# Layer-2 projections of a two-layer decoder computed as 30 block pairs by seven half-size products, with two spills to DRAM

## The chip, the cores and the metric

One core of a Trainium2 chip runs the whole program. The metric is the device time of one execution in microseconds; lower is better. PE is the matrix engine, PEld its weight loader, DVE, ACT and POOL are the vector, scalar and GpSimd engines, SP the engine that issues most transfers.

## The reference, cut to what matters

A decoder of two layers on 512 tokens of width 2048, all in f32. Layer 1 is a sparse attention with a token indexer; layer 2 is a stick-breaking attention against one K and V made from layer 1's output `x`. Each layer ends with an output projection, a layer norm and a gated embedding. The part that the change touches:

```
kb, vb = split(x @ w_kv_b)                 # 2048 x 4096: 16 heads of 128 columns each for K and V
q, g   = split(x @ w_q_b)                  # 2048 x 4096: Q and the gate, 16 heads each
z = q k^T * 128^-0.5                       # per head, strictly causal
a = exp(log_sigmoid(z) + reverse cumsum of log_sigmoid(-z) behind it)
y = ((a @ v) * silu(g)) @ w_out_b
x = layer_norm(4^0.25 * x + y);  x = x + (p @ w_ple) * sigmoid(x @ w_ple_gate)
```

## The kernel before, in words

Activations are held transposed: 16 tiles `xT[m]` of 128 features by 512 tokens. To keep f32 accuracy each operand is split in two fp32r parts, a high one (`h`, `wh`, a rounded copy by ACT) and a low one (`l`, `wl`, the rest, by DVE), and every product is three matmuls, high by high, high by low, low by high (`mm3`, lines 88 to 93). A matmul of the projections has a 128x128 block of weights loaded first and then 512 columns of tokens.

The projections are a list of chunks. A chunk is one weight tile `raw` of 128x1024 (512 KB), loaded by SP, split into `wh` and `wl` (`split_w`, L161 and L162), and used by 24 matmuls. There are 4 `raw` buffers and 3 pairs of `wh` and `wl`. At the start of chunk c the program issues the split of chunk c+2 and the load of chunk c+6 (`ahead`). A block (`block`) is two columns of 128 weights, that is two heads' worth or a head's K and Q: 4 chunks, 96 matmuls, two PSUM tiles of 128x512 in `g` buffers. `natural_block` makes V for four heads with tokens on the partitions: 8 chunks.

In layer 2 (lines 767 to 794) the loop over 16 heads emits for each four heads one `natural_block` for V, for each two heads a block for the gates, and for each head a block for K and Q. When the results are done, `b_done` splits them. The attention of a head is queued (`slots`) and one piece is taken out after each chunk: `stick_tile` for four tiles of 128 queries (scores on PE, two sigmoids on ACT, two triangular masks on POOL, a scan and a product on DVE), ten transposes (L441), and the product with V, whose gated result `u[h]` stays on chip until the output projection `mix_out(1)`. The 16 tiles `xT[m]` of layer 1's output stay on chip as `h` and `l` for the whole of layer 2; `out_done` adds them back from there. All order is fixed by the program text: each engine takes its instructions in that order and waits on semaphores.

Of the kernel before, what the change touches and what calls it, by code (L numbers as in the profile page):

```python
# [12 lines left out]
P = 128  # L13
# [18 lines left out]
RAW_BUFS = 4  # L32
HL_BUFS = 3
T_BUFS = 78

# [10 lines left out]
class Chunk:  # L46
    def __init__(self, loads, mms, pre=None, after=None, pops=1):
        self.pops = pops
        self.mid = None
        self.loads = loads  # L50
        self.mms = mms
        self.pre = pre
        self.after = after


class Kernel:
    def __init__(self, tc, pools):
# [23 lines left out]
    def split(self, src, w=T, lo=0):  # L81
# [4 lines left out]
        return h, l  # L86

# [60 lines left out]

    def load(self, c):
        if c < len(self.chunks):  # L150
            ch = self.chunks[c]
            ch.raw = self.raw.tile([P, 1024], F32, tag="raw", name=self.name("raw"))
            ch.loads(ch.raw)

    def split_w(self, c):
        if c < len(self.chunks):
            ch = self.chunks[c]
            nc = self.nc
            ch.h = self.hl.tile([P, 1024], F32R, tag="wh", name=self.name("wh"))
            ch.l = self.hl.tile([P, 1024], F32R, tag="wl", name=self.name("wl"))  # L160
            nc.scalar.copy(ch.h, ch.raw)  # L161
            nc.vector.tensor_tensor(ch.l, ch.raw, ch.h.bitcast(F32), op=OP.subtract)  # L162
            ch.raw = None

    def ahead(self, c):
        self.split_w(c + HL_BUFS - 1)
        self.load(c + RAW_BUFS + HL_BUFS - 1)

    def run(self):
        self.prologue()  # L170
        for c in range(len(self.chunks)):
# [4 lines left out]
            if ch.pre:  # L176
                ch.pre()
            for n, (off, out, xs) in enumerate(ch.mms):
# [25 lines left out]
def body(tc, x, p, positions, w_in_a, w_out_a, w_q_b, w_kv_b, w_out_b, ln_g, ln_b, w_ple, w_ple_gate, freq, out):  # L204
    nc = tc.nc
    with tc.tile_pool(name="const", bufs=1) as const, \
            tc.tile_pool(name="raw", bufs=RAW_BUFS) as raw, \
            tc.tile_pool(name="hl", bufs=HL_BUFS) as hl, \
            tc.tile_pool(name="t", bufs=T_BUFS) as tp, \
            tc.tile_pool(name="psum", bufs=1, space=bass.MemoryType.PSUM) as psum, \  # L210
            tc.manual_schedule():
        k = Kernel(tc, (const, raw, hl, tp, psum))
# [4 lines left out]
def _emit(k, x, p, positions, w_in, w_out_a, w_q, w_kv, w_out_b, ln_g, ln_b, w_ple, w_gate, freq, out):  # L217
# [43 lines left out]
    pos = const.tile([P, T], F32, name="pos")  # L261
# [171 lines left out]
    def tail(h, a):  # L433
# [16 lines left out]
        def stage_v():  # L450
            o = k.ps("o")
            sl = slice(a["col"] * P, (a["col"] + 1) * P)
            for j in range(NT):
                vh, vl = a["v"][j]
                k.mm3(o[:, j * P:T], (vh[:, sl], vl[:, sl]), a["pt"][j], j == 0, j == NT - 1)
# [64 lines left out]

    def q_done_a(h, i, ps):
        a = att.setdefault(h, {"p": [None] * NT})
        if i == 0:
            rope(ps, st[0], 64, lambda r: a.__setitem__("q", k.split(r)))
            a["k"], a["v"], a["col"] = kx[h // 4], va, h // 4
# [14 lines left out]
    def prologue():  # L540
        for n in range(RAW_BUFS):
            load_x(n)
            k.load(n)
            if n == 1:
                load_small()
        for n in range(RAW_BUFS, 8):
            load_x(n)
        first_x(range(2))
        k.split_w(0)
        k.load(RAW_BUFS)  # L550
        k.split_w(1)
        k.load(RAW_BUFS + 1)
# [115 lines left out]

    def ln_apply(layer, ms):
# [38 lines left out]
    def mix_out(layer):  # L708
# [4 lines left out]
        for n, (b, kc) in enumerate(order):  # L713
            if b not in outs:
                outs[b] = [Out(KT, lambda ps, m=2 * b + i: out_done(m, ps)) for i in range(2)]
            pre = None
            if n == 6:
                pre = finish
            if n == 0:
                k.chunks[-3].after = lambda: us_ahead(0)  # L720
                k.chunks[-2].after = lambda: us_ahead(1)
            k.chunks.append(k.chunk4(view, (2 * b * P, (2 * b + 1) * P), kc, outs[b], us, pre=pre, pops=1))
            if n in (1, 5):
                k.chunks[-1].after = lambda n=n: us_ahead(2 if n == 1 else 3)
# [30 lines left out]

    def x1_fin(m, v):
        xT[m] = k.split(v)
# [4 lines left out]

    mix_out(0)
    ple_chunks(0)
    gate_block(0, x1_fin)

    def b_done(h, what, ps):
        a = att.setdefault(100 + h, {"p": [None] * NT})
        if what == "g":
            sg = k.tt(s="sg")  # L770
            nc.scalar.activation(sg, ps, AF.Sigmoid)
            nc.vector.tensor_tensor(sg, sg, ps, op=OP.mult)
            a["g"] = sg
            return
        a[what] = k.split(ps)
        if what == "q":
            a["v"], a["col"] = vb[h // 4], h % 4
            slots(a, h, stick_tile)

    def b_load(h):  # L780
        def loads(raw, kc):
            r = raw.rearrange("p (k c) -> p k c", k=4)
            nc.sync.dma_start(r[:, :, 0:P], wkv_v[:, 4 * kc:4 * kc + 4, h * P:(h + 1) * P])
            nc.sync.dma_start(r[:, :, P:2 * P], wq_v[:, 4 * kc:4 * kc + 4, h * P:(h + 1) * P])

        return loads
# [11 lines left out]
    def out_fin(m, v):  # L798
        k.defer(lambda: out_store(m, v))
# [48 lines left out]
```

## Time and profile before

| | |
|---|---|
| median of 3 runs | 2180.03 us (2179.91 to 2180.98) |
| the profiled execution | 2180.3 us, its span 2178.5 us |
| PE busy, share of the span | 99%, 10081 matmuls |
| weight loads busy | 83% |
| DVE, ACT, POOL busy | 52%, 38%, 8% |
| DMA, mean | 92 GB/s |
| granted PE clock | 9 tenths or more in all 40 slices |

A matmul's row lasts longer than the distance to the next row's start, since matmuls overlap in the engine: what a matmul costs a stream is the distance of starts, not its length. In the projections of layer 2, from 1064 to 1815 us of the span, PE has no idle time in the windows view.

### The profile page before, as it was taken

To read this page: it belongs to the slowest core of one execution; us is meant where nothing else is said; L and a number is where in the kernel's file an instruction comes from. 1 tells how busy PE (TensorE), PEld (TensorE's weight loads), DVE (VectorE), ACT (ScalarE), POOL (GpSimd) and SP (SyncE) were. 2 spreads that over 40 slices of the span, in tenths; PEclk is the share of its full clock that TensorE was granted. 3 is DMA by queue.
4 is the path that set the end of the run, shared out by engine and by line. 5 is a ranking of instruction groups with operands and counts; after the bars stand their busy time and mean duration, and the time that the engine had idled before them with its cause. 6 is when DMAs were issued, how large, how long until landed. Compare 5 with 4: busy or idle time off the path is not lost.

```text
span 2178.5 us, 25725 instructions
## 1 busy us (share of the span) xinstructions
PE 2159.6 (99%) x10081; PEld 1803.0 (83%) x10081; DVE 1141.0 (52%) x1759; ACT 824.6 (38%) x1271; POOL 170.1 (8%) x227
## 2 busy tenths in 40 slices
PE   8999999999999999999999999999999999999999
PEld 7987888888888887888888888888888888887887
DVE  4576976555566458543344434434443456548532
ACT  3564345455553236332233323322332343226322
POOL 6101000000001010000010000100000010100000
PEclk9999999999999999999999999999999999999999
DMA  6333332223222322333323222232233222332431
GB/s 199 107 90 84 99 86 78 78 74 82 78 88 88 100 93 78 107 97 97 97 78 97 87 87 87 79 96 86 80 94 90 88 87 88 96 98 76 125 117 58
DMA packets 263946, 201.21 MB, mean 92 GB/s; under 512 B 12752, under 2 KB 251408, under 8 KB 263824
## 3 DMA queue, kind: packets, MB, share of 16 engines
q1 hardware_dynamic: 263824, 199.56, 30.4%
q8 instruction: 79, 1.29, 0.2%
q14 instruction: 43, 0.35, 0.1%
HBM read 195.33 MB, written 4.19 MB: 92 GB/s over the span
## 4 chain that ended last, share of the span: by engine, by line
PE 94%; DVE 3%; ACT 1%; issue 0%; DMA 0%; SPq 0%; ACTq 0%
PE g L91 29%; PE g L93 29%; PE g L92 29%; PE s L441 2%; PE s L91 1%; PE o L93 1%; PE o L92 1%; PE s L93 1%; PE s L92 1%; PE o L91 1%; DVE z L674 1%; PE s L375 1%; DVE z L673 1%; DVE wl L162 1%; ACT wh L161 0%
## 5 line engine op out<-in xcount | busy, mean ns | idle before, releaser
L91 PE MATMUL g<-h,wh 128*128 128x512 f32 (+1 forms) x2576 | 1003.9, 390 | 3.4 <-ACT h L84 3.4
L92 PE MATMUL g<-l,wh 128*128 128x512 f32 (+1 forms) x2576 | 997.3, 387 | 3.6 <-DVE l L85 3.6
L93 PE MATMUL g<-h,wl 128*128 128x512 f32 (+1 forms) x2576 | 997.2, 387 | 0.5 <-DVE wl L162 0.5
L162 DVE TENSOR_TENSOR wl<-raw,wh 128x1024 fp32r<-128x1024 f32 x362 | 448.6, 1242 | 503.5 <-ACT wh L161 501.1
L91 PEld LDWEIGHTS g<-h,wh 128*128 128x128 f32 x2576 | 484.2, 188 | 103.3 <-ACT h L84 5.4
L92 PEld LDWEIGHTS g<-l,wh 128*128 128x128 f32 x2576 | 484.2, 188 | 99.9 <-DVE l L85 5.9
L161 ACT CAST wh<-raw 128x1024 fp32r<-128x1024 f32 x362 | 380.1, 1054 | 492.8 <-PE g L92 384.8
L93 PEld LDWEIGHTS g<-h,wl 128*128 128x128 f32 x2576 | 483.9, 188 | 97.0 <-DVE wl L162 1.0
L91 PE MATMUL g<-wh,h 128*128 128x512 f32 x320 | 126.5, 395 | 2.1 <-ACT wh L161 2.1
L92 PE MATMUL g<-wl,h 128*128 128x512 f32 x320 | 125.2, 391 | 0.5 <-DVE wl L162 0.5
L93 PE MATMUL g<-wh,l 128*128 128x512 f32 x320 | 125.3, 392 | 0.0
L513 POOL TENSOR_SCALAR_AFFINE_SELECT keep<-keep 128x128 f32<-128x128 f32 x64 | 20.1, 314 | 931.3 <-ACT keep L509 772.1
L85 DVE TENSOR_TENSOR l<-s,h 128x512 fp32r<-128x512 f32 (+1 forms) x116 | 64.7, 611 | 50.5 <-ACT h L84 50.5
L509 ACT ACTIVATE keep<-s 128x128 f32<-128x128 f32 (+1 forms) x64 | 28.2, 441 | 159.0 <-PE s L93 157.8
L516 DVE TENSOR_TENSOR_SCAN r<-keep,zeros 128x127 f32<-128x127 f32 (+1 forms) x64 | 54.6, 853 | 56.4 <-POOL keep L513 56.4
L501 ACT ACTIVATE pr<-pr,s 128x128 f32<-128x128 f32 (+1 forms) x64 | 36.2, 566 | 125.9 <-DVE s L500 125.6
L84 ACT CAST h<-s 128x512 fp32r<-128x512 f32 (+1 forms) x116 | 54.2, 539 | 64.6 <-PE s L278 31.7
L318 POOL TENSOR_TENSOR rb<-rb,sin 128x512 f32<-128x512 f32 (+2 forms) x29 | 36.0, 1240 | 475.4 <-ACT rb L316 320.2
L91 PEld LDWEIGHTS g<-wh,h 128*128 128x128 f32 x320 | 60.5, 189 | 14.6 <-ACT wh L161 2.5
L92 PEld LDWEIGHTS g<-wl,h 128*128 128x128 f32 x320 | 60.5, 189 | 13.2 <-DVE wl L162 1.0
L93 PEld LDWEIGHTS g<-wh,l 128*128 128x128 f32 x320 | 60.4, 189 | 12.7
L85 DVE TENSOR_TENSOR l<-g,h 128x512 fp32r<-128x512 f32 x52 | 35.9, 691 | 60.6 <-ACT h L84 60.6
(151 smaller groups left out, 1633.7 us busy)
## 6 DMA issues: line engine op xcount, KB each, us to landing
raw<-in_w_in_a_dram SPq DMA_DIRECT2D x132, 256.0 KB, 3.2
raw<-in_w_ple_gate_dram SPq DMA_DIRECT2D x64, 512.0 KB, 3.5
raw<-in_w_in_a_dram SPq DMA_DIRECT2D x32, 512.0 KB, 4.1
raw<-in_w_out_a_dram SPq DMA_DIRECT2D x32, 512.0 KB, 3.5
raw<-in_w_kv_b_dram SPq DMA_DIRECT2D x32, 512.0 KB, 3.7
raw<-in_w_q_b_dram SPq DMA_DIRECT2D x32, 512.0 KB, 3.7
raw<-in_w_kv_b_dram SPq DMA_DIRECT2D x64, 256.0 KB, 2.9
raw<-in_w_q_b_dram SPq DMA_DIRECT2D x64, 256.0 KB, 3.3
```

The source lines that it names most:

```text
L84: nc.scalar.copy(h[:, lo:w], src[:, lo:w])
L85: nc.vector.tensor_tensor(l[:, lo:w], src[:, lo:w], h.bitcast(F32)[:, lo:w], op=OP.subtract)
L91: nc.tensor.matmul(out, ah, bh, start=start, stop=False)
L92: nc.tensor.matmul(out, ah, bl, start=False, stop=False)
L93: nc.tensor.matmul(out, al, bh, start=False, stop=stop)
L161: nc.scalar.copy(ch.h, ch.raw)
L162: nc.vector.tensor_tensor(ch.l, ch.raw, ch.h.bitcast(F32), op=OP.subtract)
L318: nc.gpsimd.tensor_tensor(b[:rows, col:], b[:rows, col:], sin[:rows, col:], op=OP.mult)
L441: nc.tensor.transpose(banks[b][:, off + (i - j) * P:off + (i - j + 1) * P], a["p"][i][:, j * P:(j + 1) * P], ident)
L501: nc.scalar.activation(pr[:, :n], pr[:, :n], AF.Exp, bias=mx, scale=1.0, accum_out=sm)
L509: nc.scalar.activation(keep[:, :n], ps[:, :n], AF.Sigmoid, scale=-SCALE)
L516: nc.vector.tensor_tensor_scan(r[:, 0:n - 1][:, ::-1], keep[:, 1:n][:, ::-1], zeros.to_broadcast([P, n - 1]), 1.0, op0=OP.mult, op1=OP.add)
```

## The change

The 30 pairs of 128-column blocks (16 K with Q for heads 0 to 15, two pairs of gates for heads 0 to 3, 12 V with gate for heads 4 to 15) are each computed by a scheme of seven products instead of eight (`quads`). The contraction is cut in even and odd feature tiles, the tokens in two halves of 256. Each product is one chunk of 24 matmuls of 256 columns (8 feature tiles, three matmuls each). Its weight tile is a sum of up to four quarter blocks, built in place in a `raw` buffer: four quarters are loaded by SP, two additions per pair are made by accumulating transfers that POOL issues (`add_load`), and two by DVE (`add_plus`). The token side's sums are made once from layer 1's output by `make_forms` and kept on chip as fp32r forms `F` (seven of them, 8 tiles each); an eighth, A21, serves only the one V block for heads 0 to 3, which stays a `natural_block` of its own kind (`natural_halves`). The products are added up in three PSUM tiles A, B and E, with three additions on DVE and four copies on ACT per pair. V of heads 4 to 15 comes out transposed and is turned by four PE transposes per head (`b_values`).

To make room, layer 1's output is stored to DRAM after it is made (`x1_store`) and loaded again for the residual, two tiles per block of `mix_out(1)` (`x1_load`), and `u[h]` of heads 0 to 13 is stored (`u_store`) and loaded in the last pair (`u_load`). `raw` has 6 buffers, and `plan` sets when each split, addition and load is issued. The attention of a head is no longer queued but tied to given products of the next pairs. The output tiles are stored one chunk later (`defer_by(1, ...)`).

```diff
-RAW_BUFS = 4
+HALF = T // 2
+RAW_BUFS = 6
+KEEP_U = 14
+LOAD_LEAD = 6
+ADD_LEAD = 5
...
+    def multiply(self, ch, ps, xs, start, stop):
+        nc = self.nc
+        for j in range(KT // 2):
+            wh, wl = (z[:, j * P:(j + 1) * P] for z in (ch.h, ch.l))
+            xh, xl = xs(j)
+            for n, (a, b) in enumerate(((wh, xh), (wl, xh), (wh, xl))):
+                nc.tensor.matmul(ps[:, :HALF], a, b, start=start and j == 0 and n == 0,
+                                 stop=stop and j == KT // 2 - 1 and n == 2, skip_group_check=True)
...
+        def after7(q):
+            q.setdefault("s17", None) or q.__setitem__("s17", self.tt(s="s17"))
+            nc.scalar.copy(q["s17"][:, HALF:], q["E"][:, :HALF])
...
+        def after2(q):
+            q["o1"] = self.tt(s="o1")
+            nc.vector.tensor_tensor(q["o1"][:, :HALF], q["s17"][:, :HALF], q["B"][:, :HALF], op=OP.add)
...
+            product(q, "P7", "S3", "E", True, False, after7, fresh=(1, c2), add=(0, c2))
+            if last:
+                product(q, "P1", "A11", "A", True, False, after1, fresh=(0, c1))
+                third(last)
+            product(q, "P6", "S2", "A", False, False, after6, grown=q["P7"], plus=q["P1"])
+            product(q, "P2", "A12", "B", True, True, after2, fresh=(1, c1))
+            product(q, "P4", "A22", "E", False, True, after4, grown=q["P6"], plus=q["P2"])
+            product(q, "P5", "S1", "A", False, False, after5, add=(0, c2), grown=q["P1"])
+        third(qs[-1])
...
+    def add_load(self, c):
+        ch = self.chunks[c]
+        if ch.grown is not None:
+            ch.raw = ch.grown.raw
+        self.nc.gpsimd.dma_start(ch.raw.rearrange("p (k c) -> p k c", k=8), ch.add, accum_op=OP.add)
+
+    def add_plus(self, c):
+        ch = self.chunks[c]
+        ch.raw = ch.grown.raw
+        self.nc.vector.tensor_tensor(ch.raw, ch.raw, ch.plus.raw, op=OP.add)
...
+            ch.split_at = c - HL_BUFS + 1
...
+                ev(c - LOAD_LEAD - (2 if ch.add else 0), 3, c, self.load)
...
+                t = max(ch.grown.split_at, ch.plus.split_at)
+                assert t < ch.split_at
+                ev(t, 1, c, self.add_plus)
...
+            if ch.add and ch.grown is None:
+                ev(c - ADD_LEAD, 2, c, self.add_load)
+            elif ch.add:
+                ev(ch.grown.last[0], 2, c, self.add_load)
...
+        if m in x1:
+            nc.vector.scalar_tensor_tensor(z, x1.pop(m), ALPHA, ps, op0=OP.mult, op1=OP.add)
...
-        if what == "q":
-            a["v"], a["col"] = vb[h // 4], h % 4
-            slots(a, h, stick_tile)
...
-    for h in range(HEADS):
-        if h % 4 == 0:
-            vb[h // 4] = {}
-            k.natural_block(wkv_v, D + h * P, xs, lambda t, ps, v=vb[h // 4]: v_done(v, t, ps))
-        if h % 2 == 0:
-            k.block(wq_v, (D + h * P, D + (h + 1) * P), xs, lambda i, ps, h=h: b_done(h + i, "g", ps))
-        k.block(None, b_load(h), xs, lambda i, ps, h=h: b_done(h, "kq"[i], ps))
...
+        if a == "v":
+            qs[n]["P5"].then(lambda h=ha: b_values(h))
+        if a != "k":
+            continue
+        qs[n + 1]["P2"].then(lambda h=ha: b_att(h, 0, 1))
+        qs[n + 1]["P4"].then(lambda h=ha: b_att(h, 2, 3))
+        if n + 2 < len(qs):
+            qs[n + 2]["P1"].then(lambda h=ha: b_tail(h, 0))
+            qs[n + 2]["P6"].then(lambda h=ha: b_tail(h, 1))
```

On PE, a stretch of a layer-2 block before: two PSUM tiles `g` in turn, weights `wh` and `wl` of one chunk, tokens `h` and `l`.

```order
L91 MATMUL g_12039<-h_7448,wh_11937 128x512
L92 MATMUL g_12039<-l_7449,wh_11937 128x512
L93 MATMUL g_12039<-h_7448,wl_11938 128x512
L91 MATMUL g_12043<-h_7448,wh_11937 128x512
L92 MATMUL g_12043<-l_7449,wh_11937 128x512
L93 MATMUL g_12043<-h_7448,wl_11938 128x512
```

The end of product P5 of a V and gate pair now, the four transposes of V, and the start of the next pair's P7; `f` is a form.

```order
L192 MATMUL g_13683<-f_8763,wh_13778 128x256
L192 MATMUL g_13683<-f_8763,wl_13779 128x256
L192 MATMUL g_13683<-f_8763,wh_13778 128x256
L1035 MATMUL s_13937<-ident,o_2420_13807 128x128 x4
L192 MATMUL g_13950<-f_8451,wh_13841 128x256
L192 MATMUL g_13950<-f_8451,wl_13842 128x256
L192 MATMUL g_13950<-f_8451,wh_13841 128x256
```

Each matmul is half as wide, one `wh` and `wl` set now serves 24 of these, and the V transposes stand between two products.

On DVE, the third and fourth tile of one head's attention before (`r` and `beta`), among the splits `wl` of following chunks and the splits `l` of K and Q results.

```order
L162 TENSOR_TENSOR wl_12480<-raw_12305,wh_12479 128x1024
L515 MEMSET r_12515 128x1
L516 SCALAR_TENSOR_TENSOR r_12515<-keep_12513,zeros 128x383
L518 TENSOR_TENSOR beta_12514<-beta_12514,r_12515 128x384
L515 MEMSET r_12531 128x1
L516 SCALAR_TENSOR_TENSOR r_12531<-keep_12529,zeros 128x511
L518 TENSOR_TENSOR beta_12530<-beta_12530,r_12531 128x512
L162 TENSOR_TENSOR wl_12542<-raw_12336,wh_12541 128x1024
L162 TENSOR_TENSOR wl_12572<-raw_12366,wh_12571 128x1024
L85 TENSOR_TENSOR l_12590<-g_12406,h_12589 128x512
```

The same tiles now: `wl` of the next pair's P7, the addition after P4, the tiles, `wl` of the next P1, the addition that makes the weights of P6, and the addition after P5.

```order
L300 TENSOR_TENSOR wl_13274<-raw_13053,wh_13273 128x1024
L245 TENSOR_TENSOR o_2336_13239<-o_2332_13208,g_13084 128x256
L683 MEMSET r_13310 128x1
L684 SCALAR_TENSOR_TENSOR r_13310<-keep_13308,zeros 128x383
L686 TENSOR_TENSOR beta_13309<-beta_13309,r_13310 128x384
L683 MEMSET r_13326 128x1
L684 SCALAR_TENSOR_TENSOR r_13326<-keep_13324,zeros 128x511
L686 TENSOR_TENSOR beta_13325<-beta_13325,r_13326 128x512
L300 TENSOR_TENSOR wl_13337<-raw_13147,wh_13336 128x1024
L292 TENSOR_TENSOR raw_13053<-raw_13053,raw_13147 128x1024
L241 TENSOR_TENSOR o_2332_13208<-s_2320_13109,g_13115 128x256
```

Between two `wl` splits there now stand the PSUM additions and the weight addition beside the tiles.

On POOL, one head's eight masks before.

```order
L513 AFFINE_SELECT keep_12451<-keep_12451 128x128
L513 AFFINE_SELECT beta_12452<-beta_12452 128x128
L513 AFFINE_SELECT keep_12467<-keep_12467 128x128
L513 AFFINE_SELECT beta_12468<-beta_12468 128x128
L513 AFFINE_SELECT keep_12513<-keep_12513 128x128
L513 AFFINE_SELECT beta_12514<-beta_12514 128x128
L513 AFFINE_SELECT keep_12529<-keep_12529 128x128
L513 AFFINE_SELECT beta_12530<-beta_12530 128x128
```

Now, the last two masks of a head, four accumulating transfers (P5 and P7 of two following pairs in turn), and the next head's first four masks.

```order
L681 AFFINE_SELECT keep_12756<-keep_12756 128x128
L681 AFFINE_SELECT beta_12757<-beta_12757 128x128
L287 DMA raw_12579<-in_w_q_b_dram 128x8x128
L287 DMA raw_12774<-in_w_q_b_dram 128x8x128
L287 DMA raw_12902<-in_w_q_b_dram 128x8x128
L287 DMA raw_13053<-in_w_q_b_dram 128x8x128
L681 AFFINE_SELECT keep_13245<-keep_13245 128x128
L681 AFFINE_SELECT beta_13246<-beta_13246 128x128
L681 AFFINE_SELECT keep_13261<-keep_13261 128x128
L681 AFFINE_SELECT beta_13262<-beta_13262 128x128
```

Between the masks of two heads POOL now issues four transfers.

## Rows read from the trace of the kernel before

**Rows 1.** Page, parts 1, 2 and 4: busy engines, granted clock, chain by engine.

```profile
PE 2159.6 (99%) x10081; PEld 1803.0 (83%) x10081; DVE 1141.0 (52%) x1759; ACT 824.6 (38%) x1271; POOL 170.1 (8%) x227
PEclk9999999999999999999999999999999999999999
...
PE 94%; DVE 3%; ACT 1%; issue 0%; DMA 0%; SPq 0%; ACTq 0%
```

**Rows 2.** Windows view: layer-2 projections with attention, and four heads of them.

```profile
core 0: us, PE busy (x) PEld busy (x) DVE busy (x) ACT busy (x) POOL busy (x), PEclk, DMA share, GB/s
...
1064.00:1815.00 751.00, 751.00 (x3507) 629.64 (x3506) 318.51 (x452) 234.61 (x376) 51.68 (x128) 1.00 0.29 88
1224.40:1418.40 194.00, 194.00 (x907) 162.58 (x905) 79.99 (x112) 58.27 (x93) 12.90 (x32) 1.00 0.29 87
```

**Rows 3.** Page, part 5 (form, count, busy us, mean ns, idle before): projection matmuls.

```profile
L91 PE MATMUL g<-h,wh 128*128 128x512 f32 (+1 forms) x2576 | 1003.9, 390 | 3.4 <-ACT h L84 3.4
...
L91 PE MATMUL g<-wh,h 128*128 128x512 f32 x320 | 126.5, 395 | 2.1 <-ACT wh L161 2.1
```

**Rows 4.** PE timeline (start us, length us): 28 consecutive 512-column matmuls' first and last.

```profile
1499.67 0.39 PE L93 MATMUL g<-h,wl 128*128 128x512 f32 x1
...
1505.79 0.39 PE L93 MATMUL g<-h,wl 128*128 128x512 f32 x1
```

**Rows 5.** PE timeline: narrower matmuls of one head's attention, each with own weights.

```profile
1516.68 0.33 PE L91 MATMUL o<-h,h 128*128 128x384 f32 x1
...
1517.20 0.29 PE L91 MATMUL o<-h,h 128*128 128x256 f32 x1
1517.33 0.28 PE L92 MATMUL o<-l,h 128*128 128x256 f32 x1
1517.45 0.29 PE L93 MATMUL o<-h,l 128*128 128x256 f32 x1
1517.57 0.22 PE L91 MATMUL o<-h,h 128*128 128x128 f32 x1
1517.63 0.28 PE L92 MATMUL o<-l,h 128*128 128x128 f32 x1
1517.74 0.27 PE L93 MATMUL o<-h,l 128*128 128x128 f32 x1
...
1518.36 0.28 PE L92 MATMUL s<-l,h 128*128 128x256 f32 x1
1518.48 0.28 PE L93 MATMUL s<-h,l 128*128 128x256 f32 x1
1518.60 0.40 PE L91 MATMUL g<-h,wh 128*128 128x512 f32 x1
```

**Rows 6.** Groups by form, weight loads of the same stretch's line.

```profile
L92 PEld LDWEIGHTS o<-l,h 128*128 128x128 f32 x128 | 24.0, 188 | 2.5
```

**Rows 7.** Groups by form, DVE, in the same columns as rows 3.

```profile
L162 DVE TENSOR_TENSOR wl<-raw,wh 128x1024 fp32r<-128x1024 f32 x362 | 448.6, 1242 | 503.5 <-ACT wh L161 501.1
...
L516 DVE TENSOR_TENSOR_SCAN r<-keep,zeros 128x511 f32<-128x511 f32 x16 | 20.7, 1294 | 0.0
...
L85 DVE TENSOR_TENSOR l<-s,h 128x256 fp32r<-128x256 f32 x32 | 13.3, 416 | 0.0
...
L518 DVE TENSOR_TENSOR beta<-beta,r 128x512 f32<-128x512 f32 x16 | 11.1, 693 | 1.7
```

**Rows 8.** Groups by form, POOL.

```profile
L513 POOL TENSOR_SCALAR_AFFINE_SELECT beta<-beta 128x128 f32<-128x128 f32 x64 | 34.9, 545 | 1.4
...
L288 POOL TENSOR_SCALAR t<-pos,fr 128x512 f32<-128x512 f32 x2 | 4.0, 1990 | 0.1
```

**Rows 9.** Page, part 6: loads issued by SP, KB each, median us to landing.

```profile
raw<-in_w_kv_b_dram SPq DMA_DIRECT2D x32, 512.0 KB, 3.7
...
raw<-in_w_q_b_dram SPq DMA_DIRECT2D x64, 256.0 KB, 3.3
```

**Rows 10.** View of line L143, its loads' time to landing.

```profile
DMA to landing us min/median/max: 3.5/3.8/8.6
```

More of the change, by code (lines that the diff above doesn't have):

```diff
@@ L49, in __init__ @@
         self.mid = None
+        self.grown = None
+        self.add = None
+        self.plus = None
+        self.product = None
         self.loads = loads
@@ L53, in __init__, with then, both @@
         self.after = after
+    def then(self, fn):
+        first = self.after
+        def both():
+            if first:
+                first()
+            fn()
+        self.after = both
 class Kernel:
@@ L165, in ahead @@
     def ahead(self, c):
-        self.split_w(c + HL_BUFS - 1)
-        self.load(c + RAW_BUFS + HL_BUFS - 1)
+        for _, n, fn in self.steps.pop(c, ()):
+            fn(n)
     def run(self):
+        self.plan()
         self.prologue()
@@ L177, in run @@
                 ch.pre()
+            if ch.product:
+                ch.product(ch)
             for n, (off, out, xs) in enumerate(ch.mms):
@@ L260, in _emit @@
     xT = [None] * KT
-    pos = const.tile([P, T], F32, name="pos")
+    pos = k.tt(s="pos")
     lncol = const.tile([P, 64], F32, name="lncol")
@@ L519, in stick_tile, with values @@
         a["p"][i] = beta
+    def values(v, col):
+        return [tuple(z[:, col * P:(col + 1) * P] for z in v[j]) for j in range(NT)]
     def q_done_a(h, i, ps):
@@ L761, in x1_fin, with gate_end @@
             xn.clear()
+    def gate_end(n):
+        for m in range(4 * n, 4 * n + 4):
+            xn.pop(m)
+        if n < 3:
+            x1_split(8 + 2 * n)
+            x1_split(9 + 2 * n)
     mix_out(0)
@@ new lines, in b_values, with b_att, b_tail @@
+    def b_values(h):
+        a = att[100 + h]
+        t = a.pop("vt")
+        ps = k.ps("s")
+        for i in range(NT):
+            nc.tensor.transpose(ps[:, i * P:(i + 1) * P], t[:, i * P:(i + 1) * P], ident)
+        vh, vl = k.split(ps)
+        a["v"] = [(vh[:, i * P:(i + 1) * P], vl[:, i * P:(i + 1) * P]) for i in range(NT)]
+    def b_att(h, *tiles):
+        for i in tiles:
+            stick_tile(att[100 + h], i)
+    def b_tail(h, step):
+        a = att[100 + h]
+        if h < 4:
+            a["v"] = values(vb[0], h)
+        tail(h, a)[step]()
+        if step == 1:
+            if h == 3:
+                vb.clear()
+            if h < KEEP_U:
+                k.soon(lambda: u_store(h))
@@ L796, in _emit @@
+    last = qs[-1]
+    for n, (p_name, f_name) in enumerate((("P7", "S3"), ("P1", "A11"), ("P6", "S2"), ("P2", "A12"))):
+        last[p_name].then(lambda n=n, f=f_name: (F.pop(f), u_load(range(4 * n, 4 * n + 4))))
+    last["P4"].then(lambda: us_ahead(0))
+    last["P5"].then(lambda: us_ahead(1))
+    last["P3"].then(lambda: (F.clear(), b_tail(HEADS - 1, 0)))
     outv = out.rearrange("(t p) d -> p t d", p=P)
     def out_fin(m, v):
-        k.defer(lambda: out_store(m, v))
+        k.defer_by(1, lambda: out_store(m, v))
```

244 lines of the change are left out of this document (195 added, 49 removed).

## The prediction, made before the changed kernel was run

> **What bounds the kernel now.** I read the page first. PE is busy 99% of the span and the chain that ended last runs on PE for 94% of it; the granted clock is at its upper level (2.4 GHz) in all 40 slices [rows 1]. Next the windows view: in the layer-2 projections, 1064 to 1815 us, PE is busy for 751.00 of 751.00 us, while DVE has 42%, ACT 31% and POOL 7% of it and DMA engines 29% [rows 2]. No wait ends last there; the stage is as long as its matmuls. So the price of a matmul is what counts, and the reader must not take it from the groups: a projection matmul has a mean length of 390 ns [rows 3], but 2576 x 3 of these would not fit in the span beside the rest. They overlap. The timeline shows the true distance: 27 steps from 1499.67 to 1505.79 us, 226.7 ns each [rows 4].
>
> The change makes matmuls of 256 columns, each with its own 128x128 weight load. The projections have none, but each head's attention has a few [rows 5]: three of 384 columns from 1516.68 to 1517.20, 173 ns each; three of 256 from 1517.20 to 1517.57, 123 ns each; the two that end at 1518.60, 120 ns each; 128 columns from 1517.63 to 1517.74, 110 ns. From 512 to 384 columns the distance falls by 53.4 ns; another 128 columns less gives 120 ns. At 128 columns it no longer falls in proportion: about 110 ns is a floor with a new weight load per matmul. The recorded load length is 188 ns [rows 6], so loads overlap too, or 256 columns could not go at 120. Half the columns therefore cost 53%, not 50%, of a full matmul. I take 120 ns, with 117 and 123 as bounds; the 10 ns digits of these rows allow no narrower ones.
>
> **The change part by part.** The profiled execution took 2180.3 us (span 2178.5, and 1.8 around it); the median of the runs is 2180.03, so a sum made on the one holds for the other.
>
> Removed: 30 pairs x 2 blocks x 16 feature tiles x 3 = 2880 matmuls of 512 columns, 2880 x 226.7 ns = 652.9 us, all on the path.
>
> Added: 30 pairs x 7 products x 24 = 5040 matmuls of 256 columns, 5040 x 120 ns = 604.8 us (589.7 at 117, 619.9 at 123). The algebra saves an eighth, but the width of 256 gives back half of that: 48 us net (63 to 33).
>
> Added: 12 heads x 4 transposes of V on PE, 48 x 110 ns = 5.3 us. The V block for heads 0 to 3 keeps its matmuls.
>
> DVE. Four heads took 194 us and DVE was busy for 80 of them [rows 2]. Four heads will have 56 splits `wl` for 32 (24 x 1.24 = 29.8 us), 16 weight additions of 128x1024 with two SBUF inputs, priced as `wl` (19.9), and 24 PSUM additions of 128x256 at 0.42 (10.0) [rows 7]: 140 us in 8 x 20.2 + 20 + 1.8 = 183 us, 76%. (The 20 us are the four heads' attention, 194 less 768 matmuls x 226.7 ns.) So DVE does not become the bound on average, but its order is fixed and it is late in places. A product lasts 24 x 0.12 = 2.9 us for a chunk's 5.4. With three `wh` and `wl` sets, `wl` of a product can be made only once PE has left the product three before it, and must be there 5.8 us later, where it had 10.9. The worst place is behind P4 of a V and gate pair: DVE then has the addition (0.42), two scans with their products (at most 2 x (1.29 + 0.69) = 4.0) and the `wl` of the next P1 (1.24), 5.7 us, against 5.8 plus the 1.2 us of PE scores emitted between. It starts up to 1 us late, since the two earlier tiles stand before it. I count a quarter microsecond of PE wait for each of 16 heads, 4 us, with 0 and 16 as ends. ACT gains 24 casts and 32 half-width copies per four heads from a share of 30% [rows 2]; it stays under 60%.
>
> Weights. SP loads four quarters of 512 KB per pair where it loaded as much before; its loads of that size land in 3.7 us, 256 KB in the same 512-byte runs in 3.3 [rows 9], and they are issued 4 products (11.5 us) or more before use: no cost. Two additions per pair go by accumulating transfers from POOL. No row shows one. Its nearest rows are the plain loads: 3.5 us at least and 8.6 at most [rows 10]. A gain is excluded, since POOL did nothing for weights before. P7's addition has 3 products before its split by the program, and POOL can run ahead; P5's waits for DVE's addition that makes P6 from the same buffer, which I place 3 to 4 us into P5 of the pair before, and is needed by the split five products on: 10 to 11 us. PE itself waits only when `wh` and `wl` (2.3 us) are late for the product two further on, another 3.4. So up to about 13 us from issue to landing cost nothing. I take a duration between these rows, and no wait; the cost beyond 13 us stands as a rival. By the Trainium skill, page "DMA: Bandwidth & Descriptors", section "Anatomy of one DMA — SWDGE (gpsimd) path", a transfer from GpSimd takes 2.0 us and its bytes over 436 GB/s, an estimate of 3.2 us here, without accumulation; by it this rival would be out. No row here can show it.
>
> POOL's own time to issue is unknown too: from 0.5 us (a mask [rows 8]) to 2.0 (its slowest shape here), or longer. Behind it are queued the next head's masks, behind these DVE's scans. Four transfers stand between two heads' masks, the last two within about 15 us, so under 7 us each nothing is late.
>
> Spills. Sixteen stores and loads of `x` and 14 of `u`, 256 KB each, on SP: 15 MB beside 200. DMA engines are busy for 29% [rows 2]; with 3 MB per 20 us pair, half as much again per pair in shorter time, I expect under 60%. SP's queue is not late, since loads wait no longer than the end of a product 5 or more chunks before use. The forms cost DVE and ACT some 64 half-width operations each under layer 1's gates and the V block, where both are half idle.
>
> Ends. At the last pair 16 splits of `u`, a head's tiles and V's split meet on DVE: some 13 us of work while PE has 8. I count 3 us there and 1 at the start: 4 us.
>
> Sum: 2180.3 - 652.9 + 604.8 + 5.3 + 4 + 4 = **2145.5 us**.
>
> **The rivals.** (B) *The accumulating transfers come late*, the one that ends slower. P5's or P7's weights land after more than 13 us, or POOL needs over 7 us to issue one so that the masks and DVE's FIFO behind them wait. Each microsecond past that is paid once per pair, 30 us: 16 us from issue to landing gives 3 x 30 = 90, 2236 us. The forecast's gain of 35 us is lost from 14.2 us on. For it: nothing in the trace shows the operation, and it reads and writes its target. Against it: POOL has 7% and DMA 29%. (C) *Long streams of narrow matmuls run slower than short ones.* The rows at 120 ns are runs of three, between wide matmuls that let weights and instructions be fetched ahead; 5040 in a row are not shown. At 124 ns the time is 2166, at 129 it is 2191, and at the recorded load length of 188 ns 2488. Against it: 128 columns at 110 ns several times in a row. The Trainium skill, page "TensorE: Matmul & The Clock Gate", section "Wait — 56ns, not 53.3ns?", speaks against the change: without hardware decode an instruction costs about 62 ns of sequencer time per matmul; if the weight load costs the same, 124 ns a pair, and an estimate of 2166 us. The 110 ns row is below that, but short. (D) *DVE's order holds PE in every pair*, not only in a head's tiles: 0.5 us per product triple late, 1 us per pair, 2145.5 + 30 - 4 = 2172. For it: 76% busy with half the lead. That PE's count does not fall as said is excluded by the program's order.
>
> **How the numbers follow.** Forecast 0.58 (2122 to 2165: 117 ns without any wait is 2122, 123 ns with 5 more of wait 2165). B 0.18, nearly all above 2185. C 0.12, of it 0.03 past 2185. D 0.12, 2160 to 2190. The range takes in the forecast, most of C and D, and the near end of B: 2122 to 2200; beyond lies the rest of B and C's far end, some 0.18. A measurement of this kernel can tell about 0.2% from no change, 4.4 us. Faster: the forecast's 0.58, 0.06 of C, 0.05 of D and 0.01 of B, 0.70 in all. Same: 0.03 of C and 0.03 of D, 0.06. Slower: 0.17 of B, 0.03 of C and 0.04 of D, 0.24.
>
> **What would show it.** In the trace after, 256-column starts of the projections 120 ns apart (C: 124 or more in the middle of a product). PE busy in the layer-2 stage close to its length; with B, idle PE before the first matmul of P5 or P7 and ACT `wh` waiting for a DMA; with D, PE waiting for DVE `wl` in P1, most behind a head's tiles. The stage from 1064 to 1815 should last some 716 us. The prediction is wrong if PE waits more than 1.2 us per pair.

## The result, and the profile after

| | before | after |
|---|---|---|
| median | 2180.11 us (2179.91 to 2180.98, 4 runs) | 2147.66 us (2147.24 to 2148.99, 4 runs) |
| profiled execution, its span | 2180.3, 2178.5 us | 2148.99, 2147.3 us |

The changed kernel takes 0.985 of the time before, with a 95% interval of 0.983 to 0.987: 32.5 us faster, where 34.5 were predicted.

The page after, parts 1, 2, 3 and 4, is to be set beside [rows 1]; its last lines, of parts 5 and 6, beside [rows 3] and [rows 9].

```profile
PE 2120.2 (99%) x12289; PEld 1876.8 (87%) x12289; DVE 1354.8 (63%) x2063; ACT 967.9 (45%) x1529; POOL 262.9 (12%) x287
...
PEclk9999999999999999999999999999999999999999
...
q1 hardware_dynamic: 306256, 215.29, 34.9%
q0 software_dynamic: 62400, 31.46, 11.8%
...
PE 92%; DVE 3%; issue 3%; ACT 1%; POOL 1%; DMA 0%; SPq 0%; POOLq 0%; DVEq 0%; ACTq 0%
...
L192 PE MATMUL g<-f,wh 128*128 128x256 f32 x3360 | 621.6, 284 | 5.6 <-DVE o L241 5.6
...
L292 DVE TENSOR_TENSOR raw<-raw,raw 128x1024 f32<-128x1024 f32 x60 | 73.1, 1219 | 0.0
...
raw<-in_w_kv_b_dram SPq DMA_DIRECT2D x64, 512.0 KB, 6.4
raw<-in_w_q_b_dram SPq DMA_DIRECT2D x64, 512.0 KB, 6.9
raw<-in_w_q_b_dram POOLq DMA_DIRECT2D x60, 512.0 KB, 10.3
```

PE still fills the span. The largest new idle time is one entry of 5.6 us, in front of a projection matmul, put down to DVE's line 241, which is the addition after P5.

The windows view follows, with the columns of [rows 2], for three stretches: the pairs up to head 3, four heads in the middle, and all pairs.

```profile
1056.00:1286.00 230.00, 228.07 (x1858) 225.80 (x1857) 170.36 (x229) 118.70 (x192) 47.82 (x68) 1.00 0.74 141
1286.00:1468.40 182.40, 182.40 (x1497) 181.34 (x1497) 134.80 (x177) 93.06 (x149) 38.12 (x48) 1.00 0.76 145
1055.97:1754.00 698.03, 690.51 (x5625) 685.22 (x5624) 515.32 (x682) 358.13 (x574) 142.99 (x187) 1.00 0.75 149
```

Four heads take 182.4 us where they took 194 before. PE has no gap in them; DVE is busy for 74%, ACT for 51%, DMA engines for 76%.

The PE timeline in the middle of the pairs is to be set beside [rows 4] and [rows 5]; a row with x2 holds two matmuls.

```profile
1499.84 0.28 PE L192 MATMUL g<-f,wl 128*128 128x256 f32 x1
1499.96 0.40 PE L192 MATMUL g<-f,wh 128*128 128x256 f32 x2
1500.20 0.28 PE L192 MATMUL g<-f,wl 128*128 128x256 f32 x1
...
1504.16 0.28 PE L192 MATMUL g<-f,wl 128*128 128x256 f32 x1
```

From 1499.84 to 1504.16 lie 36 steps: 120.0 ns each.

The waits of PE in the stage of the pairs (waiter, releaser, us in total, times, longest):

```profile
PE g L192 <- DVE o L241: 5.6, 1, 5.6
PE g L192 <- DVE wl L300: 1.9, 4, 0.5
```

The four short ones stand behind the tiles of heads 0 to 3. The long one is at the last pair. This is DVE's timeline there (the addition after P5 is L241):

```profile
1740.11 0.64 DVE L686 TENSOR_TENSOR beta<-beta,r 128x384 f32<-128x384 f32 x1
1740.68 1.21 DVE L684 TENSOR_TENSOR_SCAN r<-keep,zeros 128x511 f32<-128x511 f32 x1
...
1741.99 0.69 DVE L686 TENSOR_TENSOR beta<-beta,r 128x512 f32<-128x512 f32 x1
1742.60 2.49 DVE L103 TENSOR_TENSOR l<-u,h 128x512 fp32r<-128x512 f32 x4
1745.01 1.22 DVE L300 TENSOR_TENSOR wl<-raw,wh 128x1024 fp32r<-128x1024 f32 x1
1746.15 0.41 DVE L241 TENSOR_TENSOR o<-s,g 128x256 f32<-128x256 f32 x1
```

PE is through with P5 and the V transposes at 1741.1 and starts P3 at 1746.71. In between DVE is never idle: the rest of tiles 2 and 3, four splits of `u`, a `wl`, and only then the addition that frees the PSUM tile. Then the granted clock in the windows view, over this wait and over P3 behind it:

```profile
1735.00:1746.00 11.00, 6.12 (x48) 5.74 (x46) 10.58 (x21) 9.29 (x16) 4.00 (x8) 0.97 0.37 116
1746.00:1752.00 6.00, 5.29 (x25) 5.32 (x26) 4.70 (x8) 0.00 (x0) 0.00 (x0) 0.50 0.58 179
```

The clock is granted at half, 1.2 GHz; P3's matmuls step 213 ns instead of 120, and its 23 steps take 5.04 us instead of 2.76. So the wait costs 5.6 us and, by the lower clock behind it, another 2.3.

The theory to test is this: the saving is the matmuls' count times 120 ns; what is lost of it is DVE's order at the last pair and, slightly, at heads 0 to 3; the accumulating transfers and the spills are free. The rivals: the width costs more or less than 120 ns; the transfers are late here and there; DVE holds PE everywhere.

### The profile page after: what moved, and what is told of

The parts are those of the page before. It is cut to its first block, busy times and chain, and to the rows that moved or that the text cites. A ratio compares the mean times of both kernels' runs of the same rounds, so it can differ in the third digit from the quotient of the medians.

```text
span 2147.3 us, 30976 instructions
## 1 busy us (share of the span) xinstructions
PE 2120.2 (99%) x12289; PEld 1876.8 (87%) x12289; DVE 1354.8 (63%) x2063; ACT 967.9 (45%) x1529; POOL 262.9 (12%) x287
## 4 chain that ended last, share of the span: by engine, by line
PE 92%; DVE 3%; issue 3%; ACT 1%; POOL 1%; DMA 0%; SPq 0%; POOLq 0%; DVEq 0%; ACTq 0%
PE g L192 25%; PE g L118 19%; PE g L119 19%; PE g L120 19%; PE s L611 2%; PE o L119 1%; PE o L120 1%; PE o L118 1%; PE s L118 1%; PE s L119 1%; PE s L120 1%; DVE wl L300 1%; PE s L545 1%; DVE z L866 1%; DVE z L865 0%
## 5 line engine op out<-in xcount | busy, mean ns | idle before, releaser
L118 PE MATMUL g<-h,wh 128*128 128x512 f32 (+1 forms) x1808 | 704.4, 390 | 3.3 <-ACT h L102 3.3
L119 PE MATMUL g<-l,wh 128*128 128x512 f32 (+1 forms) x1808 | 698.9, 387 | 3.2 <-DVE l L103 3.2
L120 PE MATMUL g<-h,wl 128*128 128x512 f32 (+1 forms) x1808 | 698.5, 386 | 0.5 <-DVE wl L300 0.5
L192 PE MATMUL g<-f,wh 128*128 128x256 f32 x3360 | 621.6, 284 | 5.6 <-DVE o L241 5.6
L192 PEld LDWEIGHTS g<-f,wh 128*128 128x128 f32 x3360 | 530.5, 192 | 6.6 <-issue 5.8
L192 PE MATMUL g<-f,wl 128*128 128x256 f32 x1680 | 476.6, 284 | 1.9 <-DVE wl L300 1.9
L118 PEld LDWEIGHTS g<-h,wh 128*128 128x128 f32 x1808 | 340.1, 188 | 73.9 <-ACT h L102 4.8
L119 PEld LDWEIGHTS g<-l,wh 128*128 128x128 f32 x1808 | 340.4, 188 | 69.3 <-DVE l L103 4.8
L120 PEld LDWEIGHTS g<-h,wl 128*128 128x128 f32 x1808 | 340.2, 188 | 67.1 <-DVE wl L300 1.0
L192 PEld LDWEIGHTS g<-f,wl 128*128 128x128 f32 x1680 | 323.2, 192 | 3.5 <-DVE wl L300 2.7
L813 ACT ACTIVATE sq<-z 128x512 f32<-128x512 f32 x30 | 19.0, 634 | 81.6 <-DVE z L806 81.6
## 6 DMA issues: line engine op xcount, KB each, us to landing
raw<-in_w_q_b_dram POOLq DMA_DIRECT2D x60, 512.0 KB, 10.3
```

The costliest lines, as they stand in the source:

```text
L118: nc.tensor.matmul(out, ah, bh, start=start, stop=False)
L119: nc.tensor.matmul(out, ah, bl, start=False, stop=False)
L120: nc.tensor.matmul(out, al, bh, start=False, stop=stop)
L192: nc.tensor.matmul(ps[:, :HALF], a, b, start=start and j == 0 and n == 0, stop=stop and j == KT // 2 - 1 and n == 2, skip_group_check=True)
```

## The experiments

For a comparison within the stage, the span from the first to the last start of a pair matmul (L192) is given: 695.8 us in the changed kernel. The times before the stage differ by 1 to 2 us from run to run, at the first loads. The kernel before took 2181.1 us in the runs made beside the experiments (2181.7 beside the two of the plain loads), so 1.0 us (1.6) is to be taken off their times when they are set against 2147.66.

**The width alone.** The kernel before, with its matmuls in the pairs cut in two:

```diff
+        for c in (slice(0, 256), slice(256, 512)):
+            nc.tensor.matmul(out[:, c], ah, bh[:, c], start=start and c.start == 0, stop=False, skip_group_check=True)
...
```

> The kernel before, with the 2880 matmuls of 512 columns of the 30 block pairs each cut in two of 256 columns, 5760 in all, each with its own weight load: same sums, same loads, same splits. The width's price by itself. Theory (256 columns step at 120 ns against 226.7 for 512): 2880 x (240 - 226.7) = 38 us more, 2180 + 38 = 2218 us, 2210 to 2226. Rival C (long streams of narrow matmuls run slower, 124 ns or more): 2180 + 2880 x (248 - 226.7) = 2241 us or more. Rival (256 columns cost half of 512, 113.4 ns, and the algebra's saving of an eighth was lost elsewhere): 2180 us.

Measured: 2218.45 us, 37.3 us above its kernel before. Its page, part 1:

```profile
PE 2198.3 (99%) x12961; PEld 1956.0 (88%) x12961; DVE 1140.3 (51%) x1759; ACT 822.3 (37%) x1271; POOL 168.8 (8%) x227
```

and its windows view over the stage, 38 us longer than [rows 2]:

```profile
1064.00:1853.00 789.00, 789.00 (x6363) 779.97 (x6361) 318.21 (x451) 232.71 (x374) 51.42 (x128) 1.00 0.28 84
```

There are 2880 more matmuls, the other engines have the same work, and PE has no gap in the stage: 37.3 / 2880 + 226.7 = 239.7 ns for two halves, 119.8 for one. Both rivals on the width fall.

**The spills alone**, in the kernel before (stores and loads of `x1` for the residual, and of `u` for heads 0 to 11):

```diff
+            nc.vector.scalar_tensor_tensor(z, x1.pop(m), ALPHA, ps, op0=OP.mult, op1=OP.add)
...
+        nc.sync.dma_start(xd[m], v)
...
+        nc.sync.dma_start(ud[h], u[h][0])
```

> The kernel before with the spills alone: layer 1's output is stored and loaded again for the residual, and u of heads 0 to 11 is stored and loaded ahead of the output projection. Theory (the spills cost nothing, DMA engines are busy for 29% and SP is not late): the time of the kernel before within 2 us. Rival (stores and loads of 256 KB between the weight loads make these late, or the first output block waits for u): 5 us or more above it.

Measured: 2181.47 us against 2181.13, a ratio of 1.0001 (0.9992 to 1.0010). In the kernel before, where DMA engines are busy for 32% of the stage with them, the spills are free. No run takes them alone out of the changed kernel, where the share is 75%.

**No accumulating transfers.**

```diff
-        self.nc.gpsimd.dma_start(ch.raw.rearrange("p (k c) -> p k c", k=8), ch.add, accum_op=OP.add)
+        pass
```

> The changed kernel without its 60 accumulating transfers, so the weights of P7, P5 and of the two products grown from these lack a quarter block each; everything else is issued as before. Theory (the transfers land in 6.8 to 13.6 us and that lies within the slack): 2147 us, at most 2 us less; the loads by SP, which share the DMA engines, land in less than the 6.4 to 6.9 us they take now. Rival B in a weak form (a few of the transfers are late and cost PE time in sum): 5 us or more less, 2142 or below.

Measured: 2146.34 us, 2.3 us below the changed kernel after the 1.0; the ratios' intervals (0.982 to 0.986 here) overlap, so no more than that can be said. In the trace the stage is 694.0 us, 1.8 shorter, and all of that lies at the last pair: the wait there is 4.7 us instead of 5.6, and the clock behind it recovers within P3, which saves 0.9 more; heads 0 to 3 wait as before. This is page part 6 of this kernel, then its windows view of four heads and of 704 us:

```profile
raw<-in_w_kv_b_dram SPq DMA_DIRECT2D x64, 512.0 KB, 5.5
raw<-in_w_q_b_dram SPq DMA_DIRECT2D x64, 512.0 KB, 5.1
```

```profile
1286.00:1468.40 182.40, 182.40 (x1498) 181.34 (x1497) 134.80 (x177) 92.81 (x148) 12.98 (x32) 1.00 0.37 99
1056.00:1760.00 704.00, 697.44 (x5660) 690.79 (x5659) 520.46 (x688) 360.19 (x580) 50.02 (x128) 1.00 0.38 105
```

The middle of the stage lasts the same 182.40 us of PE work with and without the transfers, though DMA engines are busy for half as long. There they cost nothing. At the last pair they cost the 1.8 us, and the changed kernel's trace shows how: ACT waits for P5's transfer, the head's sigmoids stand behind this `wh` on ACT, and DVE is idle just ahead of its crowded stretch.

```profile
1733.06 1.05 ACT L299 CAST wh<-raw 128x1024 fp32r<-128x1024 f32 x1 [2.50 <-DMA raw<-in_w_q_b_dram]
1734.14 1.23 DVE L300 TENSOR_TENSOR wl<-raw,wh 128x1024 fp32r<-128x1024 f32 x1 [3.60 <-ACT wh L299]
```

**A second transfer on top.**

```diff
+        if ch.grown is not None:
+            self.nc.gpsimd.dma_start(ch.raw.rearrange("p (k c) -> p k c", k=8)[:, :2], ch.add[:, :2], accum_op=OP.add)
```

> The changed kernel with a second accumulating transfer behind each one of P5, of a quarter of its bytes (two of eight feature tiles are added twice, so the sums differ from the reference's). Theory of the prediction (costs nothing up to 13 us from issue to landing, 30 us for each us beyond): the plain 512 KB take 10.3 us, a quarter more makes about 13; 2148 to 2170 us, and PE waits, where there are any, stand before P5 with ACT wh waiting for the transfer. Rival (the slack is larger than I reckoned, since only DVE's and ACT's lead is used up): 2148 us within 2 us. Rival (POOL's own issue, 1.66 us each, is what counts): the masks come late, PE waits stand at P1 behind the tiles.

Measured: 2320.99 us, 172 us above the changed kernel after the 1.0; theory and rivals were all too low. These are POOL's and ACT's timelines for one pair, then the two largest sums of PE's waits for ACT in the stage:

```profile
1408.60 1.19 POOL L289 DMA_DIRECT2D raw<-in_w_q_b_dram  x1 [8.15 <-DMA raw<-in_w_q_b_dram]
1409.31 2.09 POOL L287 DMA_DIRECT2D raw<-in_w_q_b_dram  x1
```

```profile
1412.77 1.05 ACT L301 CAST wh<-raw 128x1024 fp32r<-128x1024 f32 x1 [5.31 <-DMA raw<-in_w_q_b_dram]
1420.99 1.05 ACT L301 CAST wh<-raw 128x1024 fp32r<-128x1024 f32 x1 [7.17 <-DMA raw<-in_w_q_b_dram]
```

```profile
PE g L192 <- ACT wh L301: 52.9, 18, 5.2
PE s L118 <- ACT beta L680: 19.7, 14, 4.6
```

The second transfer adds to the same buffer, so POOL waits some 8 us for the first to land (line L289 waited 238.5 us in 30 waits). P7's transfer of the next pair stands behind it on POOL and is issued 8 us late. ACT's `wh` at 1420.99 is P7's and waits for that one; P7's first matmul then comes 1.7 us (median) after its weights land, where it had 6.6 in the changed kernel. The `wh` at 1412.77 is P5's, and it too comes late: ACT waits for the second transfer in all 30 pairs, 158.5 us in sum, and what is queued behind it on ACT, a head's sigmoids among it, is late with it. PE is idle for 124.5 us of the stage: 58.9 before P7, 26.1 before P1, 19.7 before scores that wait for a sigmoid, 5.5 before P5. The clock is lower as well (0.94 in the stage). So this run does not price a late landing of P5 alone, as I had meant it to: 172 / 30 = 5.7 us per pair are the price of 8 us of wait in POOL's queue and of P5's later landing together, and no run separates the two.

**A plain load ahead**, into a scratch tile, without a wait; 256 KB and 512 KB:

```diff
+        if ch.grown is not None:
+            if self.scratch is None:
+                self.scratch = self.const.tile([P, 512], F32, name="scratch")
+            self.nc.gpsimd.dma_start(self.scratch.rearrange("p (k c) -> p k c", k=4), ch.add[:, :4])
```

> The changed kernel with a plain load of 256 KB into a scratch tile issued by POOL ahead of each accumulating transfer of P5 (30 of them), so that this one is issued and lands later without POOL waiting for anything. In the changed kernel wl of P5 is done 2.4 us at least, 4.1 at the median, before PE's first use, so its transfer could land that much later. Theory (the prediction's bound: nothing lost up to about 13 us from issue to landing, 30 us for each us beyond): the load costs the transfer some 1.5 us of POOL's issue and 1 to 2 us of shared DMA engines, 10.3 + 3 = 13.3 us from where it was issued; 2148 to 2165 us. Rival (the slack is used up already, what e4_extra_quarter lost is the landing itself): 90 us or more above 2148. Rival (what e4_extra_quarter lost is POOL's wait of 8 us for the first transfer, which holds the masks and P7's transfer): 2148 to 2152 here.

Measured: 2148.62 us.

> As e10_behind_half, with a plain load of 512 KB. Theory: the transfer lands some 5 us later than in the changed kernel, 1 to 2.6 us past the lead that wl of P5 had, so 30 to 80 us above 2148: 2178 to 2228. Rival (POOL's wait was what cost): 2148 to 2155. Rival (DMA engines, 75% busy without it, become the bound, 30 x 512 KB at 149 GB/s are 105 us in all): 2200 or more with PE waiting for the plain loads by SP too.

Measured: 2151.04 us. After 1.6 us for the kernel before beside them, 0.6 us less and 1.8 us more than the changed kernel; in the second trace the stage starts 2.7 us later than in the changed kernel and is itself no longer (694.9 us). These are the windows view of the second kernel over the stage, its transfers on page part 6, and POOL's timeline:

```profile
1056.00:1760.00 704.00, 696.62 (x5656) 690.14 (x5655) 520.27 (x688) 360.77 (x578) 169.69 (x216) 1.00 0.83 170
```

```profile
raw<-in_w_q_b_dram POOLq DMA_DIRECT2D x60, 512.0 KB, 10.2
```

```profile
1286.00 0.94 POOL L291 DMA_DIRECT2D scratch<-in_w_q_b_dram  x1
1291.23 3.10 POOL L292 DMA_DIRECT2D raw<-in_w_q_b_dram  x2 [4.30 <-DVE o L242]
```

DMA engines at 83% are not the bound. But the premise failed. POOL issues the load in its idle time (1286.00), before it waits for DVE ahead of P5's transfer (1291.23), so this one is issued no later; and the accumulating transfers land in 10.2 us whether or not a load goes ahead of them. So the slack was not tested, nor was a dearer issue. It stays a reading of the changed kernel's trace: P5's `wl` is done 2.4 us at least, 4.1 at the median, before PE needs it; P7's 3.3 at least.

**The last pair's splits of `u` moved.**

```diff
-    last["P4"].then(lambda: us_ahead(0))
-    last["P5"].then(lambda: us_ahead(1))
+    last["P6"].then(lambda: us_ahead(0))
+    last["P3"].then(lambda: us_ahead(1))
```

> The changed kernel with one move: of the last pair, the splits of eight u tiles that stood behind P4 now stand behind P6, and the eight behind P5 now behind P3. Theory (the 5.6 us idle time of PE at 1740.8 us is DVE's queue: the u splits and the head's tiles stand ahead of after5's addition, for which P3 waits; the matmuls behind it at about 213 ns, 256 columns at 1.2 GHz, cost some 1.4 us more): the wait goes, 2147.7 - 5.6 - 1.4 = 2141 us, 2139 to 2143. Rival (the wait is for something else that ends then too, the V split or the load of u): the wait stays 4 us or more and the time is 2146 to 2149. Second rival (the splits only move: PE now waits for h and l of u at the first output block): 2144 to 2147.

(Each of the two calls splits four tiles, not eight as written there.) Measured: 2143.97 us, 4.7 us below the changed kernel after the 1.0; the stage 3.1 us shorter, the wait 3.2 us instead of 5.6. The theory named DVE's queue rightly and its content wrongly: the four splits are 2.5 us of it, as the timeline above shows, and tiles 2 and 3 are the rest. After 3.2 us the clock still fell: 0.62 over P3, which took 4.3 us.

```profile
PE g L192 <- DVE o L241: 3.2, 1, 3.2
```

**The tiles spread, in all heads and in the last alone.** On top of the previous edit:

```diff
-        qs[n + 1]["P2"].then(lambda h=ha: b_att(h, 0, 1))
-        qs[n + 1]["P4"].then(lambda h=ha: b_att(h, 2, 3))
+        for p_name, i in (("P6", 0), ("P2", 1), ("P4", 2), ("P5", 3)):
+            qs[n + 1][p_name].then(lambda h=ha, i=i: b_att(h, i))
```

> The move of e1_end, and the four tiles of a head behind four products (P6, P2, P4, P5) instead of two behind P2 and two behind P4. Theory (heads 0 to 3 each hold PE for 0.60 to 0.66 us before P1, because wl of P1 stands on DVE behind two tiles, and from head 4 on there is next to no such wait): 4 x 0.63 = 2.5 us less than e1_end, some 2138.5 us, 2137 to 2140. Rival (the waits in the heads are the narrow matmuls' own steps, not DVE): the same time as e1_end within 0.8 us. Rival D of the prediction (DVE's order holds PE in every pair): 5 to 26 us less than e1_end.

Measured: 2150.23 us, 6.3 us above the previous kernel where less was expected; the stage 4.8 us longer. The step at the last wait is 0.7 us too long instead of 3.4, but each of the other heads lost 0.5 to 1.9 us. These are timelines of one head, POOL, ACT and then DVE:

```profile
1241.60 1.56 POOL L287 DMA_DIRECT2D raw<-in_w_q_b_dram  x1 [3.46 <-DVE r L683]
1242.52 0.96 POOL L681 TENSOR_SCALAR_AFFINE_SELECT keep<-keep 128x128 f32<-128x128 f32 x1
```

```profile
1239.77 0.60 ACT L677 ACTIVATE keep<-s 128x512 f32<-128x512 f32 x1 [1.76 <-PE s L120]
```

```profile
1241.28 0.06 DVE L683 MEMSET r<- 128x1 f32 x1
1243.51 1.29 DVE L684 TENSOR_TENSOR_SCAN r<-keep,zeros 128x511 f32<-128x511 f32 x1 [2.17 <-POOL keep L681]
```

Tile 3's mask now stands behind a transfer on POOL. Its sigmoid is done at 1240.37, but POOL stands idle until 1241.60, since that transfer waits for DVE, and then issues it for 1.56 us; DVE's scan waits 2.17 us for the mask, with `wl` behind it. That is the chain of the prediction (masks behind the transfers, DVE behind the masks), where the prediction asked for 7 us of issue: with the masks well clear of the transfers there was slack, with tile 3 behind P5 there is none. This is read from the trace; no run moves that mask alone. In the last pair no transfer stands there. Hence the same edit for head 15 alone:

```diff
+        if ha == HEADS - 1:
+            tiles = {"P6": (0,), "P2": (1,), "P4": (2,), "P5": (3,)}
```

> e1_end, with the four tiles of the last head alone behind P6, P2, P4 and P5 (one each); all other heads keep two behind P2 and two behind P4. Theory (in the run e1_end the last wait of PE is still 3.2 us, since tiles 2 and 3 of head 15 stand on DVE ahead of the addition after P5; in e6_spread, where tile 3 stands behind that addition, it is 0.7 us, and its other heads lost 12.1 - 0.7 us instead of 2.5): the last wait falls to 0.7 us, PE keeps its upper clock, so 2.5 us and some 0.8 us at the lower clock less than e1_end: 2144.0 - 3.3 = 2140.7 us, 2139.5 to 2142. Rival (the tail of the head comes late instead, in the output projection): 2143 to 2146.

Measured: 2140.74 us, as expected; the stage is 688.5 us long. These are the waits of PE in the stage, then the windows view around the last one:

```profile
PE g L192 <- DVE wl L300: 1.9, 4, 0.5
PE g L192 <- DVE r L683: 0.5, 1, 0.5
```

```profile
1735.00:1747.00 12.00, 11.46 (x84) 10.70 (x83) 11.09 (x18) 7.44 (x14) 2.32 (x5) 1.00 0.65 214
```

After half a microsecond of wait the clock did not fall: it is 1.00 from 1735 to 1747, and P3 takes 2.8 us. Last, heads 0 to 3 on top of that:

```diff
+        if ha < 4:
+            tiles = {"P6": (0,), "P2": (1, 2), "P4": (3,)}
```

> e8_last, and for heads 0 to 3 tile 0 behind P6, tiles 1 and 2 behind P2 and tile 3 behind P4. Theory (what holds PE in these four heads is wl of P1 behind tiles 2 and 3 on DVE; one tile less there takes off 0.95 + 0.64 = 1.6 us of work against waits of 0.6 to 0.65 us): the four waits go, 2.5 us less than e8_last, about 2138.2 us. Rival (the 0.5 to 0.9 us waits that e6_spread had in each head came from tile 0 or 1 at its new place, not from tile 3): heads 0 to 3 still wait 0.5 us or more, and the time is that of e8_last or above it.

Measured: 2139.66 us, ratio 0.981 (0.980 to 0.982), the lowest median of all, 8 us below the changed kernel's, 9 after the 1.0. Its interval overlaps that of the run before it (0.980 to 0.983); in the traces the stage is 1.3 us shorter, 687.2 us. The four steps that were 0.61 to 0.66 us too long are 0.27 to 0.30: half of the expected 2.5 us. DVE's timeline of one of them suggests why:

```profile
1092.72 0.41 DVE L245 TENSOR_TENSOR o<-o,g 128x256 f32<-128x256 f32 x1
1093.90 0.69 DVE L1018 SCALAR_TENSOR_TENSOR sg<-o,sg 128x512 f32<-128x512 f32 x1 [0.76 <-ACT sg L1017]
...
1094.77 1.22 DVE L684 TENSOR_TENSOR_SCAN r<-keep,zeros 128x511 f32<-128x511 f32 x1 [0.18 <-POOL keep L681]
```

The gate's product waits 0.76 us for a sigmoid that itself waits for the addition, and everything behind it on DVE with it; taking work off before that point moves nothing behind it.

## Why the prediction was right, step by step

**Matmuls: right in the step.** They were priced at 652.9 us out and 604.8 in, from 226.7 and 120 ns. The steps in the trace after are 120.0 ns in the middle of a product. The four V transposes of a head step 109 ns three times and 28 once, 0.36 us from their first start to the next product, so the 5.3 us were 4.3. Adding up all matmuls from the V block for heads 0 to 3 to the end by width, at the prices 226.7, 173, 120 and 110 ns, gives 1153.7 us before and 1110.9 after: 42.8 less, which is 48.1 less the 5.3 priced for the V transposes. This sum checks the counts; the prices are checked by the steps and by the run with cut matmuls. Two readings of the prediction were loose. It says that the width gives back half of the algebra's eighth; by its own numbers that eighth is 652.9 / 8 = 81.6 us, of which 48.1, three fifths, are left. And its floor of 110 ns at 128 columns passes over a step of 60 ns in the same rows, 1517.57 to 1517.63; neither changes the sum. Short runs of two and three matmuls in [rows 5] were enough. The groups' mean length of such a matmul, 284 ns, would again have told nothing of it.

**Waits: the size nearly right, the place wrong.** Predicted were 4 us over the heads and 4 at the ends. The trace has 2.6 us, all in heads 0 to 3, where the gates add to DVE's order; 7.9 us at the last pair (5.6 and the lower clock); nothing in heads 4 to 14. There I had placed the worst case, behind P4 of a V and gate pair. The term that was mis-sized is the last pair: I wrote 13 us of DVE work against 8 us of PE, and then took 3 us rather than the difference of 5; and I did not count what the clock takes after an idle stretch. The two errors in part cancel, 4 us for 2.6 and 4 for 7.9, and to that extent it is luck that the sum came so close.

**The accumulating transfers: right that they cost next to nothing, wrong on how close.** Their cost is 1.8 us at the last pair and nothing in the middle. They landed in 6.8 to 13.6 us, 10.3 at the median (P5's, to which the bound of 13 belongs, in 6.8 to 12.2), beyond the 3.5 to 8.6 of the plain loads [rows 10] between which I had placed them, and ACT's `wh` waited 14 times for one, 9.3 us in all. In the middle PE did not wait: it comes to P5 7.6 us (median) after the landing, 4.6 at least. The Trainium skill, page "DMA: Bandwidth & Descriptors", section "Anatomy of one DMA — SWDGE (gpsimd) path", would have it, without accumulation, at an estimated 3.2 us. The trace has three times that, and the measurement decides. The bound of 13 us and its 30 us per microsecond fit the trace but were not isolated by a run. The rival is real once POOL is held: in the run with a second transfer, 8 us of wait on POOL in front of P7's transfer and the later landing of P5 cost 5.7 us per pair.

**Loads and spills: no cost seen, but not for the reason given.** The fresh loads by SP take 6.4 to 6.9 us where I carried over 3.7 [rows 9], and DMA engines are busy for 75%, not under 60%. Neither shows as a wait of PE in the middle of the stage, and 83% cost nothing either.

**DVE, ACT, four heads: right.** DVE is busy for 74% and ACT for 51% of 182.4 us, where 76%, under 60% and 183 were predicted. A weight addition takes 1.219 us, priced at 1.24.

**The rivals.** C (narrow matmuls at 124 ns or more) is out by the rows at 120.0 ns and by the run with cut matmuls; the 124 ns, an estimate worked out from the 62 ns per matmul in the Trainium skill, page "TensorE: Matmul & The Clock Gate", section "Wait — 56ns, not 53.3ns?", do not appear. D (DVE holds PE in every pair) is out: four heads in the middle pass without any wait. B is out for this order of POOL's work, but for the 1.8 us at the last pair.

The stage length of 716 us that I named can't be compared: in the kernel before the last head's attention lay within the output projection, so that window was no whole stage. From the V block's first matmul to the last of all, 1164.4 us became 1131.0, 33.4 less. The matmuls' sum gives 42.8; the difference of 9.4 is near the 10.5 of waits and lower clock less the 1.0 that the transposes took less. The start of the program took 1.9 us longer in this execution.

## What to carry to other kernels

Price a reshaped matmul by the distance of starts of the same width in the trace, and test it by cutting the old kernel's matmuls: with halves that cost 53%, 7 products instead of 8 kept three fifths of their gain. Once PE is full, look for what is left at the seams, where the work of two phases meets on one in-order engine, and count every instruction ahead of the one that PE waits for: here the move of 8 splits and 4 tiles in one pair gave 7.3 of the 8.6 us by which the stage got shorter from the changed kernel to the last run. A move that helps one head can hurt fifteen, if another engine's queue stands differently there. A transfer that lands just in time in the steady state can still hold two engines at a seam.

## What the runs showed of the hardware that was not expected

- Accumulating transfers are dear for DMA engines: 60 of 512 KB raise the busy share of these from 38% (the run without them) to 75% of 704 us, (0.75 - 0.38) x 704 / 60 = 4.3 us of all 16 engines each, some 121 GB/s. The 30 plain loads of the same size that POOL issued on top raise it from 75% to 83%, (0.83 - 0.75) x 704 / 30 = 1.9 us each, some 279 GB/s. These are estimates from the windows view.
- Where a transfer adds to a buffer which an earlier one is still filling, the wait for the landing, 238.5 us in 30, stood on POOL itself, with everything queued behind it.
- After 5.6 and 3.2 us of idle time PE ran on at 1.2 GHz for the next 24 matmuls or part of them, 2.3 and 1.6 us lost; after 0.5 us it did not.
